# One two-bank score tile, ranked scores and joint 128-key branches in the third mixer of a two-block transformer kernel

## The chip, the cores and the metric

The kernel runs on one core of a Trainium2 chip. The metric is the device time of one execution in microseconds. The kernel before took 1426.43 us, the median of 3 runs (1425.45 to 1427.17).

## The reference, cut to what matters

The program is a chain of transformer blocks over 256 positions of width 1024 in fp32. The first block has mixers of its own. Then come two layers, each a gated feed-forward half, a mixer and a second feed-forward half. The mixer of the first of these layers is a latent attention ("second mixer"), that of the second layer is a sparse attention ("third mixer"). The change lies in the third mixer:

```python
def nsa_mixer(h, rel_bias, w_in, pos_k, w1_k, w2_k, pos_v, w1_v, w2_v, w_o):   # 16 heads, 4 key groups, 64 columns
    q, k_c, v_c, k_s, v_s, k_w, v_w, g = jnp.split(h @ w_in, cuts, axis=-1)
    kc = compress_blocks(k_c, ...); vc = compress_blocks(v_c, ...)             # 15 compressed keys
    p_cmp = softmax(q kc * scale + bias) ; o_cmp = p_cmp @ vc
    o_sel = selected_attention(q, k_s, v_s, sel_idx, tbl, scale)               # branch "s"
    o_win = window_attention(q, k_w, v_w, tbl, scale)                          # branch "w"
    o = gates[..., 0:1] * o_cmp + gates[..., 1:2] * o_sel + gates[..., 2:3] * o_win
    return o.reshape(B, S, H * NSA_V) @ w_o
```

With 256 positions all 4 blocks of 64 keys are selected and the window of 512 covers everything, so both branches "s" and "w" are causal attentions over all keys, each with its own keys and values.

## The kernel before, in words

Positions go in two tiles of 128 (t = 0, 1). Weight products are split in two fp32r parts and made as three matmuls (L227, L229, L231). Weights come by SP's DMA into `raw`, and ScalarE and VectorE split them into `wh` and `wl` (L210, L211), in a ring of four.

The third mixer (function `nsa`) first makes the keys and values of the branches (`pr_s`, `pr_w`, `ts`), then the compressed keys (`compress`, a generator that runs beside other work) and the first half of the queries, then the attention. The attention is also a generator: `pace[0] = 2` lets two of its steps be issued in program order behind each matmul of a weight product. The products beside it are `queries(1)` (the queries of heads 8 to 15) and the output product `add_out` (t = 0, then t = 1).

In program order the attention walks a list of "quads". A quad is one PSUM bank of 512 score columns and has three parts. `scores` (L1559) are fp32 matmuls with a contraction over 64 rows: even heads lie on rows 0 to 63 of the array, odd heads on rows 64 to 127. `softmax` reads the bank with VectorE (L1567: add the bias, take the extreme value), then ScalarE's exponential (L1571), a reciprocal and the gate (L1574, L1575) and a scaling (L1579). Four transposes (L384) and ScalarE's copy (L497) make `pT`, and `values` (L1588) multiplies with the values.

- At t = 0 a quad has four heads of one parity with 128 keys of one branch, at t = 1 two heads with 256 keys. A compressed quad (L1610 to L1635) comes ahead of the others of its t and half (heads 0 to 7, then 8 to 15).
- Two quads of opposite parity form a couple: their scores are issued in turns, even head, odd head (`zip`, L507). Each takes a bank from `mm`, which hands out `mm1` and `wo0` in turns, one buffer each; `po` does so with `po1` and `wo1`.
- Per half of the heads there are two couples at t = 0 and four at t = 1, 12 in all. `pr` and `pT` have four buffers.
- `mm1` and `wo0` also serve the branch products (L1472), `compress` (L1498, L1513) and t = 1 of `add_out` (L1658).

What is issued in program order isn't the order on an engine: a planner goes through the program by its own times, and gives each engine, of the instructions that are ready, the one of lowest rank. The rank is the place in program order, and `tc.high_priority(offset=n)` puts a block's ranks n lower. Each engine then runs its own list in order, and an instruction at its head that waits holds those behind it.

`attention` is also called by the first block (twice) and by the second mixer (L1373).

Of the kernel before, what the change touches and what calls it, by code (L numbers as in the profile page):

```python
# [10 lines left out]
F32 = mybir.dt.float32  # L11
F32R = mybir.dt.float32r
BF = mybir.dt.bfloat16
AF = mybir.ActivationFunctionType
OP = mybir.AluOpType
AX = mybir.AxisListType

P = 128
T = 256
# [74 lines left out]
def two_blocks_kernel(ctx: ExitStack, tc: tile.TileContext, a, cst_dram, cst2_dram, out):  # L94
    nc = tc.nc
    ve, sc, pe, gp = nc.vector, nc.scalar, nc.tensor, nc.gpsimd
# [17 lines left out]
    def tr():  # L114
        return psum.tile([P, 512], F32, name="tr", bufs=2)

    def mixer_banks(stack, *tags):

        pool = stack.enter_context(tc.tile_pool(name="mixer", bufs=2, space=bass.MemoryType.PSUM))
        return [lambda name=name, n=n: pool.tile([P, 512], F32, name=name, bufs=n) for name, n in tags]  # L120

    class Turns:

# [29 lines left out]
    def idle(n):  # L153
        for _ in range(n):
            yield
# [221 lines left out]
    def transposes(src, n, after, m=P):  # L377

        box = []

        def one(b):
            if b == 0:
                box.append(tr())
            pe.transpose(box[0][:m, b * P:(b + 1) * P], src(b), ident)  # L384
            if b == n - 1:
                after(box[0])

        return [lambda b=b: one(b) for b in range(n)]
# [26 lines left out]
    def ypair():  # L415
        h = per.tile([P, 4, T], F32R, name="yTh", bufs=2)
        l = per.tile([P, 4, T], F32R, name="yTl", bufs=2)
        return (h, l)
# [54 lines left out]
    identb = con.tile([P, P], BF)  # L473
    DECAY, CAUSAL, CAUSAL2, SLIDE = maskb[:, 0, :], maskb[:, 2, :], maskb[:, 1:3, :], maskb[:, 3:5, :]


    HEADS = (0, 2, 4, 6, 1, 3, 5, 7)

    def attention(quads, mm, pool, evac, bufs=3, couples=()):

        n = len(quads)
        pr, pT = {}, {}
        for i in range(n + 2):
            if 2 <= i:
                while i - 2 not in pT:
                    yield
                yield from quads[i - 2][2](pT.pop(i - 2))  # L490
            if 1 <= i <= n:
                p = pr.pop(i - 1)
                nb = quads[i - 1][4] if len(quads[i - 1]) > 4 else 4

                def after(pt, i=i, nb=nb):
                    pT[i - 1] = pool.tile([P, 512], F32, name="pT", bufs=bufs)
                    evac(pT[i - 1][:, :nb * P], pt[:, :nb * P])  # L497

                pending.extend(transposes(lambda b: p[:, b * P:(b + 1) * P], nb, after))
                yield  # L500
            if i < n:
                while len(quads[i]) > 3 and not quads[i][3]():
                    yield
                if i not in pr:
                    group = (i, i + 1) if i in couples else (i,)
                    banks = [mm() for _ in group]
                    for _ in zip(*[quads[g][0](s) for g, s in zip(group, banks)]):  # L507
                        yield
                    for g, s in zip(group, banks):
                        pr[g] = pool.tile([P, 512], F32, name="pr", bufs=bufs)  # L510
                        quads[g][1](s, pr[g])
# [894 lines left out]
    def nsa(xn, nxt, skew):  # L1406
        nxt.load()
        nx = ExitStack()
        pn = nx.enter_context(tc.tile_pool(name="nsa", bufs=1))
        mm1, po1, wo0, wo1 = mixer_banks(nx, ("mm", 1), ("po", 1), ("wo0", 1), ("wo1", 1))  # L1410
        mm, po = Turns(mm1, wo0), Turns(po1, wo1)
        xT = xn.x

        Bt = pn.tile([P, 16, T], F32)
# [5 lines left out]
        vbd = pn.tile([P, 4, 2, 2, 64], F32)  # L1420
        gp.memset(vbd, 0.0)
        qT = pn.tile([P, 8, T], F32)
        kT, vv = {}, {}
        gt = pn.tile([P, 2, 48], F32)


# [17 lines left out]

                pending.extend(transposes(lambda g, kv_c=kv_c: kv_c[:, g].rearrange("p a n -> p (a n)"), 4, after))

        kT["s"] = pn.tile([P, 4, T], F32, name="kTs")
        vv["s"] = pn.tile([P, 2, 256], F32, name="vs")
        kT["w"] = pn.tile([P, 4, T], F32, name="kTw")
        vv["w"] = pn.tile([P, 2, 256], F32, name="vw")  # L1450

        def ev_keys(t, p, br):
# [16 lines left out]
                sc.activation(gt[:, t, :], p[:, 256:304], AF.Tanh, scale=0.5)  # L1469
                ve.tensor_scalar(gt[:, t, :], gt[:, t, :], 0.5, 0.5, op0=OP.mult, op1=OP.add)  # L1470

        bs, bw = iter((acc, wo0)), iter((acc, mm1, wo1, po1))  # L1472
        pr_s = Product(xT, 8, w_in, 0, 1536, 512, ev_s, ps_of=lambda: next(bs)())
        pr_w = Product(xT, 8, w_in, 0, 2048, 560, ev_w, segs=[(0, 256), (256, 560)], ps_of=lambda: next(bw)())
        in_turns([(pr_s, 0), (pr_s, 1), (pr_w, 0), (pr_w, 1), (pr_w, 2)])
# [2 lines left out]
        def compress():  # L1478
            for which in range(2):
                s = "kv"[which]  # L1480
# [7 lines left out]
                ps = tr()  # L1488
# [6 lines left out]
                    ve.tensor_scalar(fl[:, j, :].rearrange("p (g n) -> p g n", g=4), c2[:, :, 2 * j:2 * j + 225:16],  # L1495
                                     posT[:, j:j + 1], None, op0=OP.add)
                yield from idle(4)
                ps = mm()  # L1498
                for j in range(16):
                    pe.matmul(ps[:, :60], w1[:, j, :], fl[:, j, :], start=j == 0, stop=j == 15)  # L1500
                    if j % 2:
# [8 lines left out]
                                 h2.rearrange("p (g n) -> p g n", g=4)[:, :, None, :].to_broadcast([P, 4, 4, 15]),  # L1510
                                 0.5, None, op0=OP.mult)
                yield from idle(16)
                ps = mm()  # L1513
                if which == 0:
                    pe.matmul(ps[:, :P].rearrange("p (g n) -> p g n", g=4), w2, hd[:, :, 0, :], start=True, stop=True)
                    for b in range(2):
                        bs = slice(64 * b, 64 * b + 64)
                        ve.tensor_copy(kcT[bs, :, b, 0:15], ps[bs, :P].rearrange("p (g n) -> p g n", g=4)[:, :, 0:15])
                else:
                    for g in range(4):  # L1520
                        pe.matmul(ps[:, g * 64:(g + 1) * 64], hd[:, g].rearrange("p r n -> p (r n)"), w2[:, 0:64],
                                  start=True, stop=True)
# [13 lines left out]
        pa = nx.enter_context(tc.tile_pool(name="nsa_attn", bufs=1))  # L1536
        add_out = AddOut(a["nsa_w_o_2"][0], [ypair(), ypair()], nxt, far=True)
        done, ready = set(), {0}

        def half(h):  # L1540
            return slice(64 * (h % 2), 64 * (h % 2) + 64)

        bank = {}

        def quad(t, bi, hh, h0):

            br = " sw"[bi]
            nb = t + 1
            nh = 4 // nb
            w = nb * P  # L1550
            j0 = 0 if t else P
            hs = hh + HEADS[h0]
            tsl = slice(t * P, (t + 1) * P)

            def scores(s):
                s = s.rearrange("p (i n) -> p i n", i=nh)
                for i in range(nh):
                    h = hs + 2 * i
                    pe.matmul(s[:, i, :], qT[half(h), h // 2, tsl], kT[br][half(h), h // 4, 0:w], start=True, stop=True)  # L1559
                    yield  # L1560

            def softmax(s, p):
                nm = small.tile([P, 4], F32, name="nm4")
                sm = small.tile([P, 4], F32, name="sm4n")
                for i in range(nh):
                    isl = slice(i * w, (i + 1) * w)
                    ve.tensor_tensor_reduce(p[:, isl], s[:, isl], Bt[:, hs + 2 * i, j0:j0 + w], 1.0, 3e38,  # L1567
                                            op0=OP.add, op1=OP.min, accum_out=nm[:, i:i + 1])
                for i in range(nh):
                    isl = slice(i * w, (i + 1) * w)  # L1570
                    sc.activation(p[:, isl], p[:, isl], AF.Exp, bias=nm[:, i:i + 1], scale=-1.0,  # L1571
                                  accum_out=sm[:, i:i + 1])
                rv = small.tile([P, 4], F32, name="rv4n")
                ve.reciprocal(rv[:, :nh], sm[:, :nh])  # L1574
                ve.tensor_mul(rv[:, :nh], rv[:, :nh],  # L1575
                              gt[:, t, :].rearrange("p (h i) -> p h i", i=3)[:, hs:hs + 2 * nh - 1:2, bi])
                for i in range(nh):
                    isl = slice(i * w, (i + 1) * w)
                    ve.tensor_scalar(p[:, isl], p[:, isl], rv[:, i:i + 1], None, op0=OP.mult)  # L1579

            def values(pT):
                for i0 in range(0, nh, 2):
                    g, k = (hs + 2 * i0 - hh) // 4, hs % 2
                    region = slice((2 * g + k) * P, (2 * g + k + 1) * P)
                    for b in range(nb):
                        for i in (i0, i0 + 1):
                            a_ = 64 * (i - i0)
                            pe.matmul(bank[t, hh][a_:a_ + 64, region],  # L1588
                                      vv[br][:, b, (hh // 4 + g) * 64:(hh // 4 + g + 1) * 64],
                                      pT[:, (i * nb + b) * P:(i * nb + b + 1) * P],  # L1590
                                      start=False, stop=bi == 2 and h0 + nh == 8 and i0 + 2 == nh and b == nb - 1)
                        yield
                if bi == 2 and h0 + nh == 8:
                    add_out.done(t, hh // 4, bank[t, hh])
                    done.add((t, hh))

            return scores, softmax, values, lambda: hh in ready

        def compressed(t, hh):
# [42 lines left out]
        def attend():  # L1642
            quads, couples = [], set()
            for hh in (0, 8):
                for t in range(2):
                    quads.append(compressed(t, hh))
                    for bi in (1, 2):
                        for h0 in range(0, 4, 4 // (t + 1)):

                            couples.add(len(quads))  # L1650
                            quads += [quad(t, bi, hh, h0), quad(t, bi, hh, h0 + 4)]
            return attention(quads, mm, pa, sc.copy, 4, couples)

        pace[0] = 2
        work = launch(attend())
        queries(1)
        ready.add(8)
        add_out((acc, acc, mm1, wo0), lambda: len(done) == 4)  # L1658
        finish(work)
        nx.close()  # L1660

# [68 lines left out]
```

## Time and profile before

| | us |
|---|---|
| median of 3 runs | 1426.43 |
| profiled execution, its own time | 1430.42 |
| span of the profiled execution | 1428.6 |
| PE busy | 1401.9 |
| DVE busy | 926.1 |
| ACT busy | 734.3 |

PE is TensorE's matmuls, PEld its weight loads, DVE is VectorE, ACT is ScalarE, POOL is GpSimd, SP is the engine whose queue issues the DMAs. A line number is a line of the kernel. Matmuls are pipelined, so the durations of neighbours overlap: what a matmul costs PE is read from its start to the start of the next one. An fp32 matmul shows as two records (two passes); `64*128` ahead of the shape is a matmul on 64 rows of the array, `128*64` one on 64 columns.

### The profile page before, as it was taken

How to read it: one execution, taken by the hardware profiler on the slowest of the kernel's cores; microseconds unless marked ns; L12 is line 12 of the kernel's file. 1: busy time of each engine (PE TensorE's matmuls, PEld its weight loads, DVE VectorE, ACT ScalarE, POOL GpSimd, SP SyncE). 2: the span in 40 equal slices, each digit the busy share in tenths (PEclk: the TensorE clock that was granted, in tenths of full speed). 3: DMA queues.
4: the chain of work that ended last, by engine and by line, in shares of the span. 5: the costliest groups of instructions: out<-in, count | busy, mean ns of one | idle time of the engine just before them, and what ended most of it. 6: DMA issues, size and time to landing. Idle time of an engine off the chain costs nothing.

```text
span 1428.6 us, 21386 instructions
## 1 busy us (share of the span) xinstructions
PE 1401.9 (98%) x8560; PEld 1219.4 (85%) x8560; DVE 926.1 (65%) x1587; ACT 734.3 (51%) x1293; POOL 46.5 (3%) x87
## 2 busy tenths in 40 slices
PE   7999999999999999999999999999999999999998
PEld 6998989999978888887788888888888977788886
DVE  5878675465577566668575656666565576676554
ACT  6646454444355454566454545545455375554543
POOL 1003000000010000110000000000000000000000
PEclk9999999999999999999999999999999899999999
DMA  7425634555546565533567655655565520455551
GB/s 255 148 88 169 217 117 148 164 173 195 177 137 232 179 205 177 164 112 129 168 208 258 211 179 190 198 186 195 189 220 188 143 60 31 132 195 189 191 192 60
DMA packets 172536, 241.77 MB, mean 169 GB/s; under 512 B 5263, under 2 KB 121748, under 8 KB 172308
## 3 DMA queue, kind: packets, MB, share of 16 engines
q1 hardware_dynamic: 172436, 240.40, 51.7%
q8 instruction: 67, 1.10, 0.3%
q14 instruction: 33, 0.27, 0.1%
HBM read 239.31 MB, written 4.22 MB: 170 GB/s over the span
## 4 chain that ended last, share of the span: by engine, by line
PE 87%; DMA 5%; DVE 3%; ACT 3%; POOL 1%; issue 1%; SPq 0%; POOLq 0%; ACTq 0%
PE acc L337 17%; PE acc L231 10%; PE acc L227 10%; PE acc L229 10%; PE acc L340 8%; PE d L231 5%; PE d L227 5%; PE d L229 5%; PE tr L384 4%; DVE wl L211 2%; DMA raw<-in_ffn_b_w_gate_dram 2%; ACT wh L210 2%; PE mm L1559 1%; PE wo L1559 1%; PE po L777 1%
## 5 line engine op out<-in xcount | busy, mean ns | idle before, releaser
L211 DVE TENSOR_TENSOR wl<-raw,wh 128x1024 fp32r<-128x1024 f32 (+5 forms) x434 | 510.6, 1199 | 228.6 <-ACT wh L210 226.7
L210 ACT CAST wh<-raw 128x1024 fp32r<-128x1024 f32 (+5 forms) x434 | 434.1, 1029 | 310.4 <-PE d L231 97.9
L337 PE MATMUL acc<-xT,wh 128*128 128x512 f32 x1152 | 398.7, 397 | 1.6 <-DVE up L345 1.4
L340 PE MATMUL acc<-xT,wl 128*128 128x256 f32 x1152 | 298.8, 280 | 0.0
L337 PEld LDWEIGHTS acc<-xT,wh 128*128 128x128 f32 x1152 | 208.0, 188 | 43.0 <-DVE up L345 2.5
L340 PEld LDWEIGHTS acc<-xT,wl 128*128 128x128 f32 x1152 | 217.1, 188 | 12.2
L227 PE MATMUL acc<-xT,wh 128*128 128x256 f32 x544 | 157.4, 289 | 0.0
L229 PE MATMUL acc<-xT,wh 128*128 128x256 f32 x544 | 157.2, 289 | 0.0
L231 PE MATMUL acc<-xT,wl 128*128 128x256 f32 x544 | 157.0, 289 | 0.0
L231 PE MATMUL d<-wh,yTl 128*128 128x512 f32 x352 | 138.0, 392 | 0.0
L227 PE MATMUL d<-wh,yTh 128*128 128x512 f32 x352 | 137.6, 391 | 0.0
L229 PE MATMUL d<-wl,yTh 128*128 128x512 f32 x352 | 137.5, 391 | 0.0
L227 PEld LDWEIGHTS acc<-xT,wh 128*128 128x128 f32 x544 | 105.2, 193 | 0.8 <-DVE y_b L471 0.3
L229 PEld LDWEIGHTS acc<-xT,wh 128*128 128x128 f32 x544 | 105.2, 193 | 0.7 <-issue 0.3
L231 PEld LDWEIGHTS acc<-xT,wl 128*128 128x128 f32 x544 | 105.2, 193 | 0.7 <-issue 0.5
L227 PE MATMUL acc<-wh,xT 128*128 128x512 f32 (+4 forms) x256 | 97.6, 382 | 0.4 <-ACT xT L405 0.4
L229 PE MATMUL acc<-wl,xT 128*128 128x512 f32 (+4 forms) x256 | 96.4, 377 | 0.0
L231 PE MATMUL acc<-wh,xT 128*128 128x512 f32 (+4 forms) x256 | 96.3, 378 | 0.0
L231 PEld LDWEIGHTS d<-wh,yTl 128*128 128x128 f32 x352 | 66.1, 188 | 15.0 <-DVE yTl L1139 0.8
L229 PEld LDWEIGHTS d<-wl,yTh 128*128 128x128 f32 x352 | 66.1, 188 | 14.0
L227 PEld LDWEIGHTS d<-wh,yTh 128*128 128x128 f32 x352 | 66.1, 188 | 13.1
L344 ACT COPY sg<-acc 128x256 f32<-128x256 f32 x72 | 26.8, 372 | 89.7 <-PE acc L337 89.4
(452 smaller groups left out, 2065.8 us busy)
## 6 DMA issues: line engine op xcount, KB each, us to landing
raw<-in_w_in_dram SPq DMA_DIRECT2D x37, 1024.0 KB, 5.0
raw<-in_ffn_a_w_gate_dram SPq DMA_DIRECT2D x22, 1024.0 KB, 5.1
raw<-in_ffn_a_w_up_dram SPq DMA_DIRECT2D x22, 1024.0 KB, 5.1
raw<-in_ffn_a_w_down_dram SPq DMA_DIRECT2D x22, 1024.0 KB, 5.0
raw<-in_ffn_b_w_gate_dram SPq DMA_DIRECT2D x22, 1024.0 KB, 5.1
raw<-in_ffn_b_w_up_dram SPq DMA_DIRECT2D x22, 1024.0 KB, 5.1
raw<-in_ffn_b_w_down_dram SPq DMA_DIRECT2D x22, 1024.0 KB, 4.9
raw<-in_w_up_dram SPq DMA_DIRECT2D x8, 1024.0 KB, 5.1
```

The source lines that it names most:

```text
L210: sc.copy(h[:, c], raw[:, c])
L211: ve.tensor_sub(l[:, c], raw[:, c], f32(h[:, c]))
L227: pe.matmul(ps, ah, bh, start=start, stop=False)
L229: pe.matmul(ps, ah, bl, start=False, stop=False)
L231: pe.matmul(ps, al, bh, start=False, stop=stop)
L337: pe.matmul(ps, h[:, k, js], pair.both(kk), start=k == 0, stop=k == nk - 1)
L340: pe.matmul(ps[:, :T], l[:, k, js], pair[0][:, kk, :], start=False, stop=False)
L344: sc.copy(d, ps[:, T:])
L384: pe.transpose(box[0][:m, b * P:(b + 1) * P], src(b), ident)
L777: pe.matmul(p[:, h * 64:(h + 1) * 64], Em[:, h, :], Vs[t][:, h, :], start=True, stop=True)
L1559: pe.matmul(s[:, i, :], qT[half(h), h // 2, tsl], kT[br][half(h), h // 4, 0:w], start=True, stop=True)
```

## The change

- The third mixer takes one tile `twin` of two banks with one buffer; every couple and every compressed quad takes the whole tile. A couple's two quads get one bank each, a compressed quad uses the first. The tile is free again when all that read either bank has run.
- The scores of a couple are issued at a rank lower by 60 in the third mixer. The other users of `attention` have an offset of 0.
- A quad of t = 0 now has two heads and both branches (the keys of the branches are one tile `kTs`): one matmul per head makes 256 columns, 128 of each branch. The couples are now: heads of one key group, even and odd. There are still two at t = 0 and four at t = 1 per half.
- `compress` takes its banks from `po`; the branch products and t = 1 of `add_out` take theirs from a `twin`.

```diff
+    def twin_banks(stack):
+        pool = stack.enter_context(tc.tile_pool(name="twin", bufs=1, space=bass.MemoryType.PSUM))
+        def take():
+            t = pool.tile([P, 2, 512], F32, name="mm")
+            return [t[:, 0], t[:, 1]]
+        return take
...
-    HEADS = (0, 2, 4, 6, 1, 3, 5, 7)
-    def attention(quads, mm, pool, evac, bufs=3, couples=()):
+    def attention(quads, mm, pool, evac, bufs=3, couples=(), twins=None):
...
-                    banks = [mm() for _ in group]
-                    for _ in zip(*[quads[g][0](s) for g, s in zip(group, banks)]):
+                    banks = twins()[:len(group)] if twins else [mm()]
+                    turns = zip(*[quads[g][0](s) for g, s in zip(group, banks)])
+                    while True:
+                        with tc.high_priority(offset=60 if twins else 0):
+                            more = next(turns, None)
+                        if more is None:
+                            break
                         yield
...
-        mm1, po1, wo0, wo1 = mixer_banks(nx, ("mm", 1), ("po", 1), ("wo0", 1), ("wo1", 1))
-        mm, po = Turns(mm1, wo0), Turns(po1, wo1)
+        twins = twin_banks(nx)
+        po1, wo1 = mixer_banks(nx, ("po", 1), ("wo1", 1))
+        po = Turns(po1, wo1)
...
-        bs, bw = iter((acc, wo0)), iter((acc, mm1, wo1, po1))
+        early = twins()
+        bs, bw = iter((acc, lambda: early[0])), iter((acc, lambda: early[1], wo1, po1))
...
-        def quad(t, bi, hh, h0):
-            br = " sw"[bi]
-            nb = t + 1
-            nh = 4 // nb
-            w = nb * P
+        def quad(t, hh, k, g, brs):
+            w = (t + 1) * P
+            n = len(brs)
             j0 = 0 if t else P
-            hs = hh + HEADS[h0]
+            hs = [hh + 4 * g + k + 2 * i for i in range(2)]
+            parts = [(i, x, slice((i * n + x) * w, (i * n + x + 1) * w)) for i in range(2) for x in range(n)]
+            b0 = brs[0] - 1
             def scores(s):
-                s = s.rearrange("p (i n) -> p i n", i=nh)
-                for i in range(nh):
-                    h = hs + 2 * i
-                    pe.matmul(s[:, i, :], qT[half(h), h // 2, tsl], kT[br][half(h), h // 4, 0:w], start=True, stop=True)
+                for i, h in enumerate(hs):
+                    pe.matmul(s[:, i * n * w:(i + 1) * n * w].rearrange("p (x m) -> p x m", x=n),
+                              qT[half(h), h // 2, tsl], kTs[half(h), b0:b0 + n, h // 4, 0:w], start=True, stop=True)
                     yield
...
-                    for bi in (1, 2):
-                        for h0 in range(0, 4, 4 // (t + 1)):
+                    for brs in ([(1,), (2,)] if t else [(1, 2)]):
+                        for g in range(2):
                             couples.add(len(quads))
-                            quads += [quad(t, bi, hh, h0), quad(t, bi, hh, h0 + 4)]
-            return attention(quads, mm, pa, sc.copy, 4, couples)
+                            quads += [quad(t, hh, k, g, brs) for k in range(2)]
+            return attention(quads, None, pa, sc.copy, 4, couples, twins)
...
-        add_out((acc, acc, mm1, wo0), lambda: len(done) == 4)
+        add_out((acc, acc, lambda: twin(0), lambda: twin(1)), lambda: len(done) == 4)
```

`softmax` and `values` loop over the same number of parts as before, now in the order head, branch. `twin(i)` takes one tile at its first call and hands out its two banks.

## Rows read from the trace of the kernel before

**Rows 1.** The page: the busy times, and the chain of work that ended last, by engine.

```profile
PE 1401.9 (98%) x8560; PEld 1219.4 (85%) x8560; DVE 926.1 (65%) x1587; ACT 734.3 (51%) x1293; POOL 46.5 (3%) x87
...
PE 87%; DMA 5%; DVE 3%; ACT 3%; POOL 1%; issue 1%; SPq 0%; POOLq 0%; ACTq 0%
```

**Rows 2.** Busy time by stretches (us from the span's start): length, PE, PEld, DVE, ACT and POOL with their instructions, granted clock as a share of 2.4 GHz, DMA share, GB/s. The stretches are the second mixer's attention, the compression, the attention of the third mixer in its first and second half, the last of the output product, and the attention as a whole.

```profile
600.00:695.00 95.00, 93.18 (x601) 76.96 (x600) 70.08 (x184) 56.59 (x146) 7.60 (x18) 1.00 0.33 111
...
1097.00:1140.00 43.00, 41.83 (x269) 38.36 (x268) 23.70 (x63) 18.48 (x28) 0.69 (x2) 0.90 0.67 172
...
1142.30:1181.60 39.30, 39.28 (x307) 29.59 (x305) 27.43 (x143) 26.77 (x87) 0.64 (x2) 1.00 0.20 55
1181.60:1223.40 41.80, 41.60 (x288) 29.00 (x286) 27.12 (x144) 25.35 (x85) 0.37 (x1) 1.00 0.08 26
1223.40:1235.30 11.90, 11.90 (x58) 9.86 (x57) 8.92 (x11) 6.37 (x10) 0.87 (x2) 1.00 0.33 96
...
1142.00:1224.00 82.00, 81.78 (x597) 59.35 (x597) 55.05 (x286) 52.60 (x173) 1.01 (x3) 1.00 0.14 40
```

**Rows 3.** Who waited for whom, PE alone, 1097 to 1240 us: us in total, times, longest.

```profile
PE wo L1500 <- DMA w<-in_nsa_cmp_w_v_dram: 0.7, 1, 0.7
PE mm L1515 <- issue: 0.3, 1, 0.3
```

**Rows 4.** The records of the score line: times, ns (least, median, most), first and last start, forms; and what VectorE's reading of the scores waited for.

```profile
L1559 PE MATMUL mm<-kTs,qT x32: 272/374/480, 1142.4 to 1208.5; 64*128 64x128 f32 x16, 64*128 64x256 f32 x16
L1559 PE MATMUL wo<-kTs,qT x32: 272/374/480, 1142.4 to 1202.2; 64*128 64x128 f32 x16, 64*128 64x256 f32 x16
L1559 PE MATMUL mm<-kTw,qT x32: 272/374/480, 1145.7 to 1215.9; 64*128 64x128 f32 x16, 64*128 64x256 f32 x16
L1559 PE MATMUL wo<-kTw,qT x32: 272/374/480, 1147.6 to 1214.4; 64*128 64x128 f32 x16, 64*128 64x256 f32 x16
...
  PE mm L1559: 4.9, 3
  PE wo L1559: 4.4, 3
```

**Rows 5.** The timeline of PE, merged: start, duration, line, operation, count. A first couple of the attention whose two parities stand in turns (16 records of 128 columns), a bank by itself (8 records), and a bank in pieces.

```profile
1142.38 0.37 PE L1559 MATMUL mm<-kTs,qT 64*128 64x128 f32 x1
1142.39 0.37 PE L1559 MATMUL wo<-kTs,qT 64*128 64x128 f32 x1
...
1143.47 0.39 PE L229 MATMUL acc<-xT,wh 128*128 128x256 f32 x1
...
1145.49 0.28 PE L231 MATMUL acc<-xT,wl 128*128 128x256 f32 x1
1145.70 1.16 PE L1559 MATMUL mm<-kTw,qT 64*128 64x128 f32 x8
1146.79 0.39 PE L227 MATMUL acc<-xT,wh 128*128 128x256 f32 x1
...
1148.36 0.48 PE L1559 MATMUL wo<-kTw,qT 64*128 64x128 f32 x2
1148.78 0.55 PE L384 MATMUL tr<-cst,pr 128*128 128x128 f32 x3
```

**Rows 6.** The same view, records of 256 columns: four in turns, then four of one bank.

```profile
1153.95 0.48 PE L1559 MATMUL wo<-kTs,qT 64*128 64x256 f32 x1
1153.95 0.48 PE L1559 MATMUL mm<-kTs,qT 64*128 64x256 f32 x1
...
1154.58 0.55 PE L384 MATMUL tr<-cst,pr 128*128 128x128 f32 x3
...
1161.57 1.13 PE L1559 MATMUL wo<-kTw,qT 64*128 64x256 f32 x4
1162.63 1.16 PE L1635 MATMUL po<-pT,vbd 128*128 128x128 f32 x8
```

**Rows 7.** The same view: the last scores, the last values, and the first matmul of t = 1 of the output product.

```profile
1215.53 0.70 PE L1559 MATMUL mm<-kTw,qT 64*128 64x256 f32 x2
1216.16 0.50 PE L227 MATMUL acc<-wh,yTh 128*128 128x512 f32 x1
...
1222.81 0.66 PE L1588 MATMUL po<-pT,vw 128*64 128x128 f32 x8
1223.40 0.50 PE L227 MATMUL mm<-wh,yTh 128*128 128x512 f32 x1
```

**Rows 8.** The timeline of VectorE: its first and last reading of the first couple (eight of 128 columns, the first and the eighth), of a couple of t = 1 (four of 256 columns, the first and the fourth), and the last reading of any score bank.

```profile
1144.15 0.28 DVE L1567 CUSTOM_DVE_ANT_0 pr<-mm,Bt 128x128 f32<-128x128 f32 x1
...
1146.53 0.26 DVE L1567 CUSTOM_DVE_ANT_0 pr<-wo,Bt 128x128 f32<-128x128 f32 x1
...
1155.79 0.42 DVE L1567 CUSTOM_DVE_ANT_0 pr<-wo,Bt 128x256 f32<-128x256 f32 x1
...
1157.48 0.42 DVE L1567 CUSTOM_DVE_ANT_0 pr<-mm,Bt 128x256 f32<-128x256 f32 x1
...
1216.82 0.42 DVE L1567 CUSTOM_DVE_ANT_0 pr<-mm,Bt 128x256 f32<-128x256 f32 x1
```

**Rows 9.** PE's waits in the feed-forward half behind the mixer, 1235 to 1300 us, as in rows 3.

```profile
PE tr L384 <- DVE xn L431: 1.4, 1, 1.4
PE acc L337 <- DVE up L345: 0.4, 1, 0.4
```

More of the change, by code (lines that the diff above doesn't have):

```diff
@@ L1422, in nsa @@
         qT = pn.tile([P, 8, T], F32)
-        kT, vv = {}, {}
+        kTs = pn.tile([P, 2, 4, T], F32, name="kTs")
+        kT, vv = {"s": kTs[:, 0], "w": kTs[:, 1]}, {}
         gt = pn.tile([P, 2, 48], F32)
@@ L1445, in ev_c @@
                 pending.extend(transposes(lambda g, kv_c=kv_c: kv_c[:, g].rearrange("p a n -> p (a n)"), 4, after))
-        kT["s"] = pn.tile([P, 4, T], F32, name="kTs")
         vv["s"] = pn.tile([P, 2, 256], F32, name="vs")
-        kT["w"] = pn.tile([P, 4, T], F32, name="kTw")
         vv["w"] = pn.tile([P, 2, 256], F32, name="vw")
@@ L1497, in compress @@
                 yield from idle(4)
-                ps = mm()
+                ps = po()
                 for j in range(16):
@@ L1512, in compress @@
                 yield from idle(16)
-                ps = mm()
+                ps = po()
                 if which == 0:
@@ L1564, in softmax @@
                 sm = small.tile([P, 4], F32, name="sm4n")
[L1565 to L1572, printed above, removed]
@@ L1573, in softmax @@
-                rv = small.tile([P, 4], F32, name="rv4n")
[L1574 to L1579, printed above, removed]
-            def values(pT):
[L1582 to L1591, printed above, removed]
+                for e, (i, x, sl) in enumerate(parts):
+                    ve.tensor_tensor_reduce(p[:, sl], s[:, sl], Bt[:, hs[i], j0:j0 + w], 1.0, 3e38,
+                                            op0=OP.add, op1=OP.min, accum_out=nm[:, e:e + 1])
@@ new lines, in softmax @@
+                for e, (i, x, sl) in enumerate(parts):
+                    sc.activation(p[:, sl], p[:, sl], AF.Exp, bias=nm[:, e:e + 1], scale=-1.0,
+                                  accum_out=sm[:, e:e + 1])
+                rv = small.tile([P, 4], F32, name="rv4n")
+                m = len(parts)
+                ve.reciprocal(rv[:, :m], sm[:, :m])
+                rv2 = rv[:, :m].rearrange("p (i x) -> p i x", i=2)
+                ve.tensor_mul(rv2, rv2, gt[:, t, :].rearrange("p (h i) -> p h i", i=3)[:, hs[0]:hs[1] + 1:2,
+                                                                                   brs[0]:brs[0] + n])
@@ new lines, in softmax @@
+                for e, (i, x, sl) in enumerate(parts):
+                    ve.tensor_scalar(p[:, sl], p[:, sl], rv[:, e:e + 1], None, op0=OP.mult)
+            def values(pT):
+                final = brs[-1] == 2 and g == 1 and k == 1
+                region = slice((2 * g + k) * P, (2 * g + k + 1) * P)
+                for x, bi in enumerate(brs):
+                    for b in range(t + 1):
+                        for i in range(2):
+                            e = (i * n + x) * (t + 1) + b
+                            pe.matmul(bank[t, hh][64 * i:64 * i + 64, region],
+                                      vv[" sw"[bi]][:, b, (hh // 4 + g) * 64:(hh // 4 + g + 1) * 64],
+                                      pT[:, e * P:(e + 1) * P],
+                                      start=False, stop=final and x == n - 1 and b == t)
@@ L1592, in values @@
                         yield
-                if bi == 2 and h0 + nh == 8:
+                if final:
                     add_out.done(t, hh // 4, bank[t, hh])
@@ L1657, in nsa, with twin @@
         ready.add(8)
-        add_out((acc, acc, mm1, wo0), lambda: len(done) == 4)
+        late = []
+        def twin(i):
+            if not late:
+                late.extend(twins())
+            return late[i]
+        add_out((acc, acc, lambda: twin(0), lambda: twin(1)), lambda: len(done) == 4)
         finish(work)
```

## The prediction

> **What bounds the kernel now.** I read the page first: PE is busy for 98% of the span, and 87% of the chain that ended last is PE [rows 1]. The question is whether that holds where the change works, so the second view is the stretches. In the attention of the third mixer, 1142 to 1224 us, PE is busy for 81.78 of 82.00 us at the full 2.4 GHz, VectorE for 55 and ScalarE for 53, and DMA moves little; both halves look alike [rows 2]. The third view is who waited: from 1097 to 1240 us PE has two waits, 1.0 us in all, neither in the attention [rows 3]. So a PE microsecond saved there is a microsecond of the span, as long as nothing else is late in its place.
>
> The timeline of PE then shows what the score line costs. It has 128 records, 64 of 128 columns and 64 of 256 [rows 4]. What is to be seen in them is that the array's two halves of 64 rows can run at once. In the first couple the records of `mm` and `wo` start in pairs 0.01 us apart, and 16 records take 1.09 us up to the next matmul; the eight records of one bank by itself, a little later, take 1.09 us as well [rows 5]. A record whose neighbour is of the other parity is free.
>
> **The price of a stretch of scores.** Two records of 128 columns by themselves take 0.42 us, eight take 1.09 [rows 5]: 0.111 us a record and 0.20 us once. Two of 256 columns take 0.63 us [rows 7], four of one bank 1.06, but four in turns 0.63 again [rows 6]: 0.215 us a record or pair of records, and again 0.20 us once. The 0.20 us falls on the change from matmuls on all rows to those on half the rows and back. There is more of it ahead of the stretch: the matmul at 1145.49 takes 0.21 us to the first score instead of the 0.107 us in which 256 columns stream at 2.4 GHz [rows 5]. I put 0.10 us there.
>
> **Before.** Going through PE's timeline I count 33 stretches of scores, the first at 1142.38 [rows 5], the last at 1215.53 [rows 7]; from the start of each to the next other matmul they take 23.7 us together. Of that 33 x 0.20 = 6.6 us are switches and 17.1 us columns; all 128 records one by one would be 64 x 0.111 + 64 x 0.215 = 20.9 us. So only some of the pairs meet today: the two banks come free at different times, and what is ready of one bank is issued alone.
>
> **After.** A couple is four matmuls, eight records of 256 columns, at t = 0 (two branches side by side) as at t = 1. There are 12 couples, so 48 pairs of records x 0.215 = 10.3 us. Since both banks come free together and the ranks are low, the four should stand together: 12 stretches make 12.7 us, two per couple 15.1 us. I take one and a half per couple, 18 stretches: 10.3 + 18 x 0.20 = 13.9 us. The gain is 23.7 - 13.9 = 9.8 us, and 15 fewer stretches x 0.10 us ahead of them give 1.5 more: 11.3 us. Of it 6.8 us are columns (17.1 - 10.3) and 4.5 us switches. The ends are 13.1 us (12 stretches: 11.0 + 21 x 0.10) and 9.5 us (24 stretches: 8.6 + 0.9).
>
> **The wait that is added.** The scores of a couple now wait until VectorE has read both banks of the couple ahead; today each bank is handed over alone. Behind a waiting score stand, in PE's list, the transposes, the values and the weight matmuls, and ScalarE's copy and the next softmax wait for these. The trace doesn't show the joint wait, so bounds: below, nothing, since VectorE is idle for 27 of 82 us [rows 2] and itself waited 9.3 us for scores [rows 4]; a gain is excluded as a wait for two banks can't end before a wait for one. Above, PE stands still while both banks are read: 1144.15 to the end of the eighth reading at 1146.8 is 2.6 us at t = 0, 1155.79 to 1157.9 is 2.1 us at t = 1 [rows 8], so 4 x 2.6 + 8 x 2.1 = 27 us. I take 1 us, near the lower end, because the rows of today's waits are there: PE, handed single banks by the same VectorE, waited for none [rows 3], and it has weight matmuls to put in between.
>
> **The rest, at nothing.** VectorE's and ScalarE's instructions keep their number and shapes. `compress` on `po`'s banks: PE's only waits there are the 1.0 us of rows 3, of which 0.7 is a DMA; the cover is that these banks were left by the branch products before `compress` needs them, and without it the price is a wait like those. t = 1 of the output product now wants both banks at once: the last reading of scores ends at 1217.2 [rows 8], the product's first matmul comes at 1223.40 [rows 7], 6 us of cover. No DMA moves in the queue; the loads of the next half wait for ring slots that the output product frees, and come earlier with it. What is late next there is the norm for t = 1: PE waits 1.4 us for it already [rows 9], relative to the product's end, so it moves along. The offset of 0 in the second mixer can change the order of equals; PE has 1.8 us of idle there [rows 2], so -1.8 to +1.8 us, and I take 0.
>
> **The sum.** 11.3 - 1.0 = 10.3 us. The profiled execution would go from 1430.42 to 1420.1 us; it lies 4.0 us above the median of the runs, and that taken off gives 1416.1 us for the median. With 9.5 to 13.1 us of gain and 0 to 4 us of wait its own range is 1412.5 to 1421.
>
> **Rivals.**
>
> *Half the pairs don't form.* The planner still issues a head of one parity, then something else. For it: today they are in turns in program order too, and most come apart. Against: that is where banks come free singly, and where both were free the couple did stand together [rows 5, 6]. With 24 of the 48 pairs apart, 24 x 0.215 = 5.2 us are lost: 1421.3 us.
>
> *The hand-over decides: slower.* One tile with one buffer makes scores, then reading, then scores. Where the planner puts the next scores at the head of PE's list just as it believes VectorE done, and VectorE is late, PE stands. For it: the lower rank takes weight matmuls out from ahead of the scores, and they were the slack. Against: PE has no wait of this kind now [rows 3], VectorE is two thirds busy [rows 2]. It decides from 11.3 / 12 = 0.94 us of idle per couple. At two thirds of the upper bound, 18 us, the time is 1426.4 - 11.3 + 18 = 1433 us. The Trainium skill (TensorEngine Tiling, Performance Considerations, on the PSUM bottleneck) warns of this side: packing speeds TensorE, not the emptying of the banks, which may then set the pace. By it the attention would take VectorE's time if that were full; the trace has 55 of 82 us there [rows 2], which even after the gain is 55 of 71, so I give the rule no more than this rival's chance.
>
> *The chain of softmaxes sets the end: no change.* From the last score at 1215.53 to the last values at 1222.81 lie 7.3 us of softmax, transposes and copy [rows 7], which don't shrink. If such latency set the length of the attention, saved PE time would come back as idle: 1426 us. Against: PE is busy throughout these 7.3 us with the product of t = 0, and the 11.9 us of t = 1 [rows 2] are behind.
>
> **How the numbers follow.** Forecast 0.58; half the pairs 0.16, 1421.3; hand-over 0.10, 1433; no change 0.10, 1426; more than worked out 0.06, below 1412. A measurement of this kernel can tell 0.2%, 2.9 us. Faster by more: 0.58 + 0.16 + 0.06 = 0.80; the no-change case with the edges of its neighbours 0.11; slower 0.09. The range of 8 in 10 leaves out the hand-over and most of the two ends: 1411 to 1425 us.
>
> **What would show it.** Right: the score line's records all of 256 columns, 96 of them, starting in pairs; 12 to 24 stretches; the attention about 10 us shorter with PE still over 99% busy. Wrong: waits of PE scores for VectorE's L1567 counterpart of more than a few microseconds, or single records of one parity between other work, or an attention shorter by 10 us while the following feed-forward half is longer by as much.

## The result, and the profile after

The changed kernel took 1415.66 us, the median of 4 runs (1414.57 to 1416.17); the kernel before took 1426.43 in the same comparison. The ratio is 0.9924, with an interval of 0.9911 to 0.9936: 10.8 us less. Predicted were 1416.1 us, and 10.3 us less. In a later comparison the changed kernel came to 0.9927 (0.9914 to 0.9940).

The page after, busy times and chain by engine [rows 1]:

```profile
PE 1387.0 (98%) x8528; PEld 1208.0 (85%) x8528; DVE 927.3 (66%) x1587; ACT 733.3 (52%) x1293; POOL 45.8 (3%) x87
...
PE 86%; DMA 4%; ACT 4%; DVE 3%; POOL 1%; issue 1%; SPq 0%; POOLq 0%; ACTq 0%; DVEq 0%
```

PE has 32 instructions less, the halved score matmuls of t = 0, and 14.9 us less busy time; VectorE and ScalarE are as before. 14.9 us is more than the runs gained, and the reason is not the change. In the profiled execution of before, PE's granted clock fell to the lower of its two levels, 1.2 instead of 2.4 GHz, just ahead of the attention: it is 1.00 from 1130 to 1131 us, while PE runs the compression's matmuls (L1500) behind a wait of 0.7 us for their weights [rows 3], 0.50 from 1132 to 1141 and 1.00 again from 1142. The stretch 1134 to 1142 us of that execution, columns as in rows 2:

```profile
1134.00:1142.00 8.00, 8.00 (x41) 8.00 (x40) 3.08 (x10) 2.21 (x4) 0.31 (x1) 0.52 0.02 4
```

Half the clock over 8 us costs some 4 us (an estimate from this row), and that execution took 4.0 us more than the median of its runs. In the kernel before profiled once more (`e5` below) the same stretch has the full clock, and so has the kernel after. I therefore compare with that second profile: its span is 1424.5 us, that of the changed kernel profiled again 1414.0, which is 10.5 us less.

The score line after [rows 4], and what its matmuls and weight loads waited for (us, times):

```profile
L1571 PE MATMUL mm<-kTs,qT x96: 376/376/481, 1139.0 to 1198.8; 64*128 64x256 f32 x96
...
  DVE rv4n L1586: 0.5, 2
  DVE rv4n L1588: 0.4, 1
  DVE pr L1591: 0.2, 1
```

96 records, all of 256 columns. The profile puts none of the waits down to VectorE's reading of the scores, L1579: L1586 and L1588 are the reciprocal and the gate, L1591 the scaling. And VectorE, which waited 9.3 us for the couples' scores before [rows 4], waits for none of them now. PE's timeline shows how they stand: a couple of t = 0 and one of t = 1, and what comes ahead of them and behind [rows 5, 6].

```profile
1138.84 0.28 PE L237 MATMUL acc<-xT,wh 128*128 128x256 f32 x1
1139.05 1.14 PE L1571 MATMUL mm<-kTs,qT 64*128 64x256 f32 x8
1140.11 0.39 PE L239 MATMUL acc<-xT,wh 128*128 128x256 f32 x1
...
1155.14 0.38 PE L1600 MATMUL wo<-pT,vw 128*64 128x128 f32 x2
1155.45 1.13 PE L1571 MATMUL mm<-kTs,qT 64*128 64x256 f32 x8
1156.51 0.43 PE L1600 MATMUL wo<-pT,vw 128*64 128x128 f32 x2
...
1198.07 1.14 PE L1571 MATMUL mm<-kTs,qT 64*128 64x256 f32 x8
1199.14 0.43 PE L1600 MATMUL po<-pT,vs 128*64 128x128 f32 x2
```

Both parities are in one tile now, so the view merges them, but the time tells that they run side by side: eight records from 1139.05 to 1140.11 are 1.06 us, where four of one parity took 1.06 [rows 6]. There are 12 such stretches, one per couple, 12.8 us together. The second one shows the price of the rank: the scores cut the values of a quad in two. A quad's eight value records take 0.59 us to the next other matmul; cut after six they take 0.58 and 0.36. Five quads are cut, four by the scores of a couple and one by compressed scores, which the rank moves as well. In all, values stand in 23 stretches and 15.0 us instead of 21 and 13.8.

Last, PE in the attention, from 1134 us to the first transposes of the norm behind the output product of t = 0. In the kernel before (second profile):

```profile
1134.00:1223.00 89.00, 88.65 (x641) 65.53 (x640) 59.51 (x296) 55.88 (x178) 2.20 (x6) 1.00 0.14 38
```

and after (second profile):

```profile
1134.00:1213.00 79.00, 77.79 (x609) 59.30 (x608) 61.02 (x298) 54.93 (x178) 2.28 (x6) 1.00 0.15 42
```

10.0 us less, 10.9 of PE's work, against 0.9 more idle (0.35 before, 1.21 after). So 10.0 of the 10.5 us have their place here. The other 0.5 us is behind: PE waits 0.9 instead of 1.4 us for the norm of t = 1.

By kind of matmul, each counted from its start to the next start, the 10.0 us are: scores 11.1 less, values 1.2 more, transposes 0.7 less, weight products 0.6 more, the rest the same. An idle time counts with the matmul ahead of it.

### The profile page after: what moved, and what is told of

It reads as the page before. It is cut to its first block, busy times and chain, and to the rows that moved or that the text cites. A ratio compares the mean times of both kernels' runs of the same rounds, so it can differ in the third digit from the quotient of the medians.

```text
span 1413.6 us, 21329 instructions
## 1 busy us (share of the span) xinstructions
PE 1387.0 (98%) x8528; PEld 1208.0 (85%) x8528; DVE 927.3 (66%) x1587; ACT 733.3 (52%) x1293; POOL 45.8 (3%) x87
## 4 chain that ended last, share of the span: by engine, by line
PE 86%; DMA 4%; ACT 4%; DVE 3%; POOL 1%; issue 1%; SPq 0%; POOLq 0%; ACTq 0%; DVEq 0%
PE acc L347 17%; PE acc L241 10%; PE acc L237 10%; PE acc L239 10%; PE acc L350 9%; PE d L241 5%; PE d L237 5%; PE d L239 5%; PE tr L394 4%; DVE wl L221 2%; ACT wh L220 1%; DMA raw<-in_ffn_b_w_gate_dram 1%; ACT pr L1582 1%; PE po L789 1%; DMA raw<-in_ffn_b_w_up_dram 1%
## 5 line engine op out<-in xcount | busy, mean ns | idle before, releaser
L220 ACT CAST wh<-raw 128x1024 fp32r<-128x1024 f32 (+5 forms) x434 | 433.8, 1029 | 308.0 <-PE d L241 95.1
L237 PE MATMUL acc<-xT,wh 128*128 128x256 f32 x544 | 156.1, 287 | 0.0
L237 PE MATMUL d<-wh,yTh 128*128 128x512 f32 x352 | 137.6, 391 | 0.0
L237 PEld LDWEIGHTS acc<-xT,wh 128*128 128x128 f32 x544 | 104.2, 191 | 0.7 <-DVE y_b L481 0.3
L237 PE MATMUL acc<-wh,xT 128*128 128x512 f32 (+4 forms) x256 | 97.4, 381 | 0.3 <-ACT xT L415 0.3
L241 PEld LDWEIGHTS d<-wh,yTl 128*128 128x128 f32 x352 | 66.1, 188 | 14.9 <-DVE yTl L1151 0.8
L237 PEld LDWEIGHTS d<-wh,yTh 128*128 128x128 f32 x352 | 66.1, 188 | 13.1
```

What stands on the lines that cost most here:

```text
L220: sc.copy(h[:, c], raw[:, c])
L237: pe.matmul(ps, ah, bh, start=start, stop=False)
L241: pe.matmul(ps, al, bh, start=False, stop=stop)
```

## The experiments

All are compared with the kernel before by ratio; at 1425.7 us, 0.001 is 1.4 us. In PE's timelines I counted the stretches of scores and summed them as for the kernel before, and took PE's idle time as length less busy time in the stretch just shown, from 1134 us to the same transposes. The kernel before has 23.9 us of scores here and 23.7 in its first profile, because its first couple took 1.27 instead of 1.09 us: its records paired one place out of step.

| kernel | ratio (interval) | stretches of scores, us | idle, us |
|---|---|---|---|
| before, again | 1 | 33, 23.9 | 0.35 |
| after, again | 0.9927 (0.9914 to 0.9940) | 12, 12.8 | 1.2 |
| e1 same parity | 0.9985 (0.9977 to 0.9994) | 12, 23.0 | 0.3 |
| e7 joint branches alone | 0.9991 (0.9982 to 1.0000) | 29, 23.9 | 0.7 |
| e2 with the two-bank tile, no rank | 1.0015 (1.0007 to 1.0024) | 29, 21.3 | 5.2 |
| e3 with the rank, single banks | 0.9966 (0.9953 to 0.9978) | 20, 19.8 | 0.9 |
| e4 tile and rank, old quads | 0.9937 (0.9923 to 0.9951) | 14, 13.9 | 1.6 |
| e9 rank 20 | 0.9977 (0.9968 to 0.9986) | 25, 20.0 | 2.6 |
| e10 rank 200 | 0.9943 (0.9931 to 0.9956) | 12, 12.8 | 0.8 |
| e6 values ranked too | 0.9923 (0.9910 to 0.9936) | 12, 12.8 | 1.7 |
| e11 values and scores at 60 | 0.9932 (0.9920 to 0.9945) | 13, 13.1 | 2.3 |

**Columns side by side, or fewer stretches?** The couples are formed of the same parity:

```diff
-                        for g in range(2):
+                        for k in range(2):
                             couples.add(len(quads))
-                            quads += [quad(t, hh, k, g, brs) for k in range(2)]
+                            quads += [quad(t, hh, k, g, brs) for g in range(2)]
```

> The changed kernel with couples of two quads of the same parity instead of opposite parity. PE's list keeps the same 12 stretches of four score matmuls, the same waits and the same other work; only the rows of the array differ, so no two records can run beside each other. My theory (most of the gain is columns that run side by side): each stretch grows from 1.06 to 0.20 + 8 x 0.215 = 1.92 us, 12 x 0.86 = 10.3 us in all, so about 1426 us, the time of the kernel before. Rival (the gain is the smaller number of stretches, or the attention follows VectorE and not PE): 1416 to 1418 us.

0.9985, 8.3 us slower than the changed kernel and still 2.1 us faster than the kernel before. The first couple in its PE timeline:

```profile
1140.05 1.99 PE L1571 MATMUL mm<-kTs,qT 64*128 64x256 f32 x8
1141.97 0.39 PE L239 MATMUL acc<-xT,wh 128*128 128x256 f32 x1
```

This stretch takes 1.92 us to the next matmul, as worked out, and so do the other eleven. So 10.3 us of columns come back, and the time grows by 2.0 us less: PE's idle falls from 1.2 to 0.3 us, which is about half of it; the other half I can't place. The rival is out. The 2.1 us that are left fit what fewer stretches are worth by the prices of the sum: 21 x 0.30 = 6.3 us, less 3.3 us of columns that met in the kernel before (23.0 - 12 x 0.20 against 23.9 - 33 x 0.20) and 1.1 us of the values (14.9 against 13.8), is 1.9.

**Tile or rank?** The rank is taken away, the banks are handed out singly (for the branch products and t = 1 of `add_out` too), and both:

```diff
-                        with tc.high_priority(offset=60 if twins else 0):
+                        with tc.high_priority(offset=0):
```

```diff
-                    banks = twins()[:len(group)] if twins else [mm()]
+                    banks = [mm() for _ in group]
...
-        po1, wo1 = mixer_banks(nx, ("po", 1), ("wo1", 1))
-        po = Turns(po1, wo1)
+        mm1, po1, wo0, wo1 = mixer_banks(nx, ("mm", 1), ("po", 1), ("wo0", 1), ("wo1", 1))
+        mm, po = Turns(mm1, wo0), Turns(po1, wo1)
```

> The changed kernel with the offset of the score ranks at 0 in the third mixer too; the two-bank tile and the joint branches stay. In PE's list the scores now stand in 29 stretches, 14 of them a single matmul. If the two-bank tile alone brought the gain, the time would stay at 1416 to 1418 us. By my prices the rank is needed as well: 17 pairs of matmuls (17 x 2 x 0.215 = 7.3 us), 14 single ones (6.0 us) and 29 switches (5.8 us) are 19 us instead of 12.8, with 17 more stretches x 0.10 ahead of them about 8 us more: 1424 us.

> The changed kernel with rank and joint branches, but the two banks handed out one by one as before (two tiles of one bank). In PE's list the scores stand in 20 stretches. If the rank alone brings the gain: 1416 to 1417 us. By my theory the common release is needed for the pairs: 8 more stretches x 0.30 = 2.4 us, and some 4 to 5 us of columns that no longer meet: 1421 to 1423 us. The other way round, should the joint wait of the two-bank tile cost much, this kernel would be faster than the changed one.

> The joint branches at t = 0 alone: single banks as before, offset 0. 29 stretches of scores in PE's list, few of them with both banks. With the two-bank tile alone the kernel took 1428 us, with the rank alone 1421. If those two each had their own price, this kernel takes about 1425 to 1426 us, like the kernel before (about 17 us of columns and 29 switches x 0.30, against 17.1 and 33 x 0.30). If the two-bank tile without a rank costs nothing by itself, and the joint branches were what made that kernel slow, this one takes 1428 us as well.

The kernel with joint branches alone, which also has `compress` on `po`'s banks, is worth 1.3 us, with an interval that reaches to nothing. It doesn't take 1428 us, so the joint branches are not what makes the kernel with the tile slow. The tile without the rank makes it 3.4 us slower (1.0015), though its scores take 2.6 us less of PE. The rank without the tile brings 3.6 us (0.9966); 1420.9 us lies just below what was expected. Tile and rank together bring 9.1 us beyond the joint branches alone (0.9927): far more than the sum, -3.4 + 3.6. The price list had 1424 us for the tile without the rank, which was wrong; it was 1428.3, and its stretch shows why:

```profile
1134.00:1225.50 91.50, 86.30 (x609) 60.12 (x607) 61.92 (x297) 55.54 (x177) 2.11 (x6) 1.00 0.13 37
```

5.2 us of idle. Who waited for whom in the same kernel, PE alone:

```profile
PE wo L1600 <- ACT pT L504: 2.0, 3, 0.9
PE mm L1571 <- DVE nm L1579: 0.9, 1, 0.9
...
PE tr L394 <- DVE pr L1591: 0.6, 2, 0.4
PE tr L394 <- DVE pr L1641: 0.5, 1, 0.5
PE mm L1571 <- DVE pr L1629: 0.5, 1, 0.5
PE mm L237 <- DVE nm L1579: 0.4, 1, 0.4
```

PE waits for the tile itself (L1571 and L237 for VectorE's readings L1579 and L1629) and for what comes late behind it, pT and pr. With single banks and no rank the idle is 0.7 us, so it comes with the joint tile; with the rank it is 1.2 us, so the rank takes most of it away. My reading is that scores issued as soon as the tile is free leave the softmax its time, and scores issued late don't. VectorE's waits for scores bear it out; in the kernel with the tile and no rank:

```profile
DVE pr L1579 <- PE mm L1571: 14.3, 6, 5.8
```

With joint branches alone it waits 7.4 us for scores, with the rank and single banks 6.5, with the tile and a rank of 20 6.9, in the changed kernel and with a rank of 200 not at all. So without the rank the tile's scores come late and the softmax waits for them. That PE's 5.2 us of idle follow from this, softmax by softmax, is argued and not shown.

With the rank but single banks, a couple can stand together as in the first of these two and cost 1.07 us, or mostly bank by bank as in the second and cost 1.62:

```profile
1149.66 0.48 PE L1569 MATMUL wo<-kTs,qT 64*128 64x256 f32 x1
1149.67 0.48 PE L1569 MATMUL mm<-kTs,qT 64*128 64x256 f32 x1
...
1150.73 0.44 PE L1598 MATMUL wo<-pT,vs 128*64 128x128 f32 x4
...
1153.68 0.91 PE L1569 MATMUL wo<-kTs,qT 64*128 64x256 f32 x3
1154.27 0.45 PE L1569 MATMUL mm<-kTs,qT 64*128 64x256 f32 x1
...
1155.30 0.44 PE L1598 MATMUL wo<-pT,vs 128*64 128x128 f32 x4
```

**How far must the rank reach?** Offsets of 20 and 200 instead of 60:

> The changed kernel with the offset of the score ranks at 20 instead of 60. 25 stretches of scores in PE's list, 16 matmuls without a partner. By my prices 32 x 0.43 + 25 x 0.20 = 18.8 us of scores instead of 12.8 and 13 x 0.10 more ahead of them: 7.3 us slower than the changed kernel, 1423 us, if PE waits no more than there. If PE's idle time comes with scores that are late, as at offset 0 (5.2 us of idle between 1134 us and the first norm transposes, against 1.2), up to 4 us on top: 1427 us.

> The changed kernel with an offset of 200. 12 stretches of scores as at 60, 26 of values instead of 23. If a rank further ahead only cuts the values into more pieces: 3 x 0.30 = 0.9 us slower, 1416 us. If scores too far ahead leave PE waiting for the bank, 1418 us or more.

At 20 the scores stand in 25 stretches and the kernel is 7.1 us slower than the changed one. The 7.3 us of the prices hit, but partly by luck: the scores take 7.2 us more (20.0, where 18.8 were worked out), idle is 1.4 us more (2.6), and the values, which are no longer cut, take 1.3 us less (21 stretches, 13.7 us). At 200 it is 2.3 us slower, between the two times that were expected, and the two intervals overlap a little. It has the same 12 stretches of scores, no more idle in the attention, and 26 stretches of values (16.0 us against 15.0). 1.0 us are the values. More than the rest is lost ahead of the attention in its profiled execution, which took 1418.73 us, the longest of its five:

```profile
PE tr L394 <- ACT kv_c L1448: 1.8, 1, 1.8
```

The changed kernel waits 0.2 us there. ScalarE makes `kv_c` behind a weight split (L220) that waited 3.8 us for its DMA, where in the changed kernel it waited 2.2 us. Whether the rank has any part in that late DMA is open, so no more than the 1.0 us is shown to be the price of reaching too far.

**Are the joint branches worth anything?** The quads of the kernel before (`quad`, `HEADS` and the loops of `attend`) stand in the changed kernel:

> Two-bank tile and rank with the quads of the kernel before: at t = 0 four heads with 128 keys of one branch, 64 records of 128 columns instead of 32 of 256. 14 stretches. By my prices 32 pairs x 0.111 = 3.6 us against 16 x 0.215 = 3.4 us, and two stretches x 0.30 more: 0.8 us slower than the changed kernel, 1416 to 1417 us. Rival (the joint 256-column matmuls are a main part of the gain, because a short matmul doesn't cover its weight load): 1419 us or more.

0.9937, 1.4 us slower than the changed kernel by ratios whose intervals overlap. A couple of 16 records of 128 columns costs hardly more than eight of 256: here from 1139.05 to the next matmul it is 1.10 us, there 1.06.

```profile
1139.05 1.16 PE L1574 MATMUL mm<-kTs,qT 64*128 64x128 f32 x16
1140.15 0.39 PE L239 MATMUL acc<-xT,wh 128*128 128x256 f32 x1
```

What there is lies in the order: 14 stretches instead of 12, 13.9 us instead of 12.8, and 0.4 us more idle. The rival, a price of the short matmuls themselves that made them a main part of the gain, is out.

**The clock.** The kernel before, profiled once more:

> The kernel before, unchanged, profiled once more. Its first profiled execution had a granted clock of 0.52 of 2.4 GHz from 1134 to 1142 us and lay 4 us above the median of its runs, which I take to be one thing, by chance and not due to the kernel. If so, this execution has the full clock there, and 1425 to 1427 us. If the kernel before always lost the clock there, it shows 0.5 again at 1425 us, and part of the gain of the change would be the clock.

```profile
1134.00:1142.00 8.00, 7.87 (x70) 7.37 (x70) 6.06 (x22) 2.92 (x8) 0.31 (x1) 1.00 0.10 20
```

1426.24 us, and 70 matmuls in the stretch at the full clock where the first profile had 41 at half. The kernel before doesn't always lose the clock, and the gain of the change isn't the clock.

**Can the values be gathered too?** `values` gets a rank as well, by the same construction as the scores:

```diff
-                yield from quads[i - 2][2](pT.pop(i - 2))
+                turns = quads[i - 2][2](pT.pop(i - 2))
+                while True:
+                    with tc.high_priority(offset=60 if twins else 0):
+                        more = next(turns, turns)
+                    if more is turns:
+                        break
+                    yield
...
-                        with tc.high_priority(offset=60 if twins else 0):
+                        with tc.high_priority(offset=75 if twins else 0):
```

> The changed kernel with the values of a quad ranked lower by 60 as well, and the scores by 75. In PE's list the scores stand in 12 stretches as in the changed kernel, the values in 17 instead of 23. If a stretch of other tiling costs 0.20 us and some 0.10 ahead of it, as the scores had it, the six that go are worth 1.8 us: 1413 to 1414.5 us beside 1415 us. Rival: values at a lower rank come before their data are there, and PE waits for ScalarE's copies: 1416 us or more.

> Values and scores both ranked lower by 60: 13 stretches of scores, 16 of values instead of 12 and 23. 6 stretches fewer x 0.30 = 1.8 us of PE's time. With 75 for the scores the same sum came out as 1.0 us less PE time and 0.5 us more idle, 0.5 us in all and inside the interval. I expect the same here, 1414.5 to 1416 us; a gain of 1.5 us would say that PE's idle there came from the scores' lead over the values.

The values come in 17 and 16 stretches, 13.9 us instead of 15.0, but idle rises from 1.2 to 1.7 and 2.3 us. So the 1.8 us that were worked out for `e6` didn't come: 1.1 us less of values, half of it idle again. 0.9923 and 0.9932 can't be told apart from 0.9927, and none of the kernels tried is shown to be faster than the changed one.

The changed kernel, unchanged, for these comparisons:

> The changed kernel, unchanged, beside the others on the same chip: 0.9924 of the kernel before, 1414.5 to 1416 us.

## Why the prediction was right, point by point

**What bounds.** PE, as read; of the 10.9 us of work that PE lost in the attention 10.0 us came out there, and 10.5 us of the span. The norm for t = 1 behind the mixer moved along and a little more: PE waits 0.9 us for it in the second profile after, 1.4 in the second before, as [rows 9]. The offset of 0 in the second mixer changed nothing that can be seen: in the second profiles the compression's first matmul (L1500, then L1513) starts at 1117.66 us before and 1117.63 after.

**The prices.** 0.215 us for a pair of records of 256 columns and 0.20 us once per stretch hold where a stretch is all pairs or has no pair: 8 x 0.215 / 2 + 0.20 = 1.06, and all 12 stretches took 1.06; without partners 8 x 0.215 + 0.20 = 1.92, and all 12 took 1.92. Stretches in which only some records meet lie between, as the 1.62 us above.

**The number of stretches was mis-sized.** I took one and a half per couple; it was one. The scores took 12.8 us instead of the 13.9 of the sum, and there are 21 fewer stretches instead of 15. With 0.10 us ahead of each this term is 23.9 - 12.8 + 2.1 = 13.2 us, the upper end I had (13.1), not 11.3. The 0.10 us was read at a single place, and it was too much for the average stretch: transposes, weight products and the rest, where it has to show, came out even with 0.9 us more idle among them, so it was about 0.9 us instead of 2.1.

**A term was missing.** Ranked scores go between the values of other quads. The values have no term in the sum; what it puts at nothing there is VectorE's, ScalarE's and `compress`'s part, and PE's values aren't named. Their number is the same, their stretches are not: 23 instead of 21, 1.2 us more. This took back most of what the term above had too little, so it is in part luck that the forecast came within 0.5 us of the measured gain.

**The wait.** 1.0 us was taken, 0.9 us more idle was measured. Of the waits that the profile lists in the attention, 0.3 us is at scores and 0.6 us at values and transposes that wait for `pT` and `pr`. The row on which I based it (no waits today) was a poor reason, though: without the rank the same joint tile costs 4.5 us of idle beyond the single banks (5.2 against 0.7). That the rank takes it away was not in the sum at all; I had put the rank on the side of the risk, as that which takes the slack from ahead of the scores.

The sum with the measured terms: 11.1 for the scores and 0.9 around them, less 1.2 and 0.9, is 9.9 us, beside the 10.0 by which the attention became shorter; the 0.5 us of the norm come on top.

**Signs and ends.** The records, the stretches and the length came as written under what would show it right, but PE is busy for 77.79 of 79.00 us of the stretch, 98.5% and not over 99%. And the lower end of the sum's own range doesn't follow from its terms: 1426.4 - 13.1 is 1413.3 us, not 1412.5.

**The rivals.** Half the pairs apart: what the scores look like with single banks or a rank of 20, with times near the one given (1420.9 and 1422.3 us beside 1421.3), but not in this kernel. The slow hand-over: real, and it decided where the rank was missing, 1428.3 us, with 5.2 us of idle, a fifth of the upper bound of 27 us. Of these 1.8 us are waits for the tile itself, the mechanism that was named; the others are for `pT` and `pr`. The condition was the reverse of the one I gave: the lower rank takes the wait away. No change, through the chain of softmaxes: not so, although ScalarE's exponentials (L1582) now make 14.8% of the chain of the attention, where the kernel before had none of them among its first dozen entries: what is taken from PE next may meet them, which no run here shows. The rule of the Trainium skill that the prediction quoted (TensorEngine Tiling (Array Packing), Performance Considerations), that emptying the banks may set the pace, did not decide here: VectorE is busy for 61 of 79 us.

## What to carry to other kernels

In these traces matmuls on different rows of the array ran side by side only where they were neighbours in PE's list, and a list built by readiness made them neighbours where they became ready together: give the partners one release (one tile over both banks) and a rank that gets them issued at that moment. Either alone is worth less or is a loss here (the tile 3.4 us slower, the rank 3.6 faster, both together 9.1 faster), so a trial of the tile alone would have thrown the idea away. And count the switches of tiling as work of their own, also those that a ranked group causes in others.

## What the runs showed of the hardware that was not expected

A stretch of matmuls on half the rows costs 0.20 us beyond its columns whatever its length (1.06 and 1.92 us with eight records, 0.62 to 0.63 with two), which made 33 stretches cost 6.6 us. A partner on the other rows is free to within 0.01 us per stretch if the two start together (eight records in pairs 1.06 us, four of one parity 1.06), also for fp32 and with two records per matmul. And two profiles of one and the same kernel can differ by 4 us in one stretch through the granted clock alone (41 matmuls in 8 us at 0.52, 70 at 1.00): a difference of two profiles of this size is to be checked against the medians before it is explained.
